# Attention weights split once, early, and reloaded as two parts

## The chip, the cores and the metric

The kernel runs on one core of one Trainium2 chip. The metric is device time in microseconds (us) of one execution. Engines are called as in the profile: PE (TensorE, its matmuls), PEld (its weight loads), DVE (VectorE), ACT (ScalarE), POOL (GpSimd) and SP (SyncE, which here only issues DMAs). A line such as L112 is line 112 of the kernel before.

## The reference

One step of a small decoder trunk, on 16 meta tokens plus 1,024 prompt tokens and on 8 sample tokens, 1,024 features wide, all in fp32:

```
hp = layer_norm(ALPHA * hp + pool_mixer(hp));   hp = layer_norm(ALPHA * hp + conv_ffn(hp))   # layer 0
k, v = hp @ w_kv + b_kv                                                                      # shared keys, values
q = x @ w_q + b_q                      # 16 heads of 64, 4 kv heads, window of 128, one sink per head
e = exp(s - m);  p = e / (sum(e) + exp(sink - m));  y = (p @ v) @ w_o + b_o
hp = layer_norm(ALPHA * hp + y);                hp = layer_norm(ALPHA * hp + conv_ffn(hp))   # layer 1

conv_ffn: g, u = split(x @ w_in);  c = conv_b + sum_k g[shifted by k] * conv_w[k];  (silu(c) * u) @ w_out
```

D_FF is 2,816, that is 22 tiles of 128. Layer 0 mixes by pooling, layer 1 by the attention.

## The kernel before

Activations lie feature-major: 8 tiles of 128 features, and columns for tokens in three chunks (280, 384 and 384 columns). Full precision on PE is had by exact parts: a matrix `w` is kept as `w_hi`, rounded to fp32r, and `w_lo = w - w_hi`, and a product is three matmuls, hi*hi, hi*lo and lo*hi (`mm3`, L115 to L122).

Weights arrive unsplit. `load_w` (L103) loads 128x1024 fp32 (512 KB) into a staging tile `raw` (two buffers), ACT rounds it into the upper half of a tile `w` (L111, CAST), and POOL subtracts to make the lower half (L112). Tiles `w` have four buffers, tiles `wo` two. With `pieces=2` both steps are done in two halves of 512 columns. All ConvFFN weights and all attention weights come this way: 2 for keys, 2 for values, 24 loads of query weights (8 head pairs in each of 3 chunks), and 24 loads of output weights (8 in each of 3 chunks).

The ConvFFN (L354) runs over tiles f = 0..21. `ffn1(f, c)` makes gate and value products of one chunk on PE (L365, L367); ACT copies the gate out of PSUM (L376, L390); POOL makes the first term of the convolution (L378, L392); DVE adds the other terms (L393, L394); ACT takes Silu (L398); DVE multiplies (L399); ACT rounds and DVE subtracts for the parts of `h` (L401, L402). After every second f, `ffn2` (L405) multiplies two tiles of h by two output weights into 8 sums per chunk, and DVE adds each PSUM bank into `acc` (L417 to L420). Six PSUM banks serve both.

The attention (L589 to L862) runs units of 128 queries of one head pair: scores, masked minimum on DVE (L645), exp on ACT (L647), normalization on DVE (L650), transposes, split (L660, L661), and the product with the values (L676 to L683). Beside them run the query projection of the next head pair (L607, with four small SBUF-to-SBUF DMAs `q<-q`, L623 and L628) and the output projection of the chunk (`pz`, L757).

The order of the instructions on each engine is made by a planner: it simulates the program with its own costs and places every instruction when its simulated engine and operands come free. On the chip each engine then works strictly in that order, waiting on semaphores. All DMAs are issued by SP, in SP's order.

Of the kernel before, what the change touches and what calls it, by code (L numbers as in the profile page):

```python
# [7 lines left out]
F32 = mybir.dt.float32  # L8
# [19 lines left out]
# prompt blocks (of 128 tokens) per chunk; the first chunk also carries the  # L28
# meta tokens and the sample tokens: columns [meta 16 | samples 8 | prompt]
# [6 lines left out]
# columns alive after the attention: [meta14 meta15 | samples 8 | prompt]  # L36
# [3 lines left out]
# packed per-partition constant columns  # L40
# [7 lines left out]
# constants of the first phase alone  # L48
# [11 lines left out]
def trunk_kernel(ctx: ExitStack, tc: tile.TileContext, ins: dict, outs: dict):  # L60
# [19 lines left out]
    # ------------------------------------------------------------ constants  # L80
# [33 lines left out]

    def mm3(out, wts, movs):  # L115
        """out += sum_k w_k^T x_k over exact hi/lo parts (all but lo*lo)."""
        n = len(wts)
        for k in range(n):
            (wh, wl), (mh, ml) = wts[k], movs[k]
            nc.tensor.matmul(out, lhsT=wh, rhs=mh, start=(k == 0), stop=False)  # L120
            nc.tensor.matmul(out, lhsT=wh, rhs=ml, start=False, stop=False)  # L121
            nc.tensor.matmul(out, lhsT=wl, rhs=mh, start=False, stop=(k == n - 1))  # L122
# [7 lines left out]
    # ----------------------------------------------------------- layer norm  # L130
    def colsum(parts, W, name, on_pe, own=False, split=False, pairs=False, step=KT):
        """mean over all features of 8 [P, W] tiles -> PSUM, on every partition; pauses after every step tiles."""
        ps = bank(f"ps_{name}", "ln")[:, :W]
        if on_pe:
            # fp32 products; with pairs, of sums of two tiles
            n = KT // 2 if pairs else KT
            for k in range(n):
                if pairs:
                    t = hslot([P, W], f"pr{k}_{name}", F32)
                    (nc.gpsimd if k < n // 2 else nc.vector).tensor_tensor(t, parts(2 * k), parts(2 * k + 1), ALU.add)  # L140
                else:
                    t = parts(k)
                nc.tensor.matmul(ps, lhsT=r32(ones), rhs=t, start=(k == 0), stop=(k == n - 1))
            return ps
        s = [None, None]
        for m in range(0, KT, 2):
            # two chains of sums, so that one is ready while the other's last ends
            i = m // 2 % 2
            a, b = parts(m), parts(m + 1)
            eng = nc.vector if split and i else nc.gpsimd  # L150
            if s[i] is None:
                s[i] = a if own else ltmp([P, W], f"s{i}_{name}")
                eng.tensor_tensor(s[i], a, b, ALU.add)
            else:
                eng.tensor_tensor(s[i], s[i], a, ALU.add)
                eng.tensor_tensor(s[i], s[i], b, ALU.add)
            if (m + 2) % step == 0 and m + 2 < KT:
                yield
        s, s1 = s
        nc.gpsimd.tensor_tensor(s, s, s1, ALU.add)  # L160
        sh = ltmp([P, W], f"sh_{name}", F32R)
        sl = ltmp([P, W], f"sl_{name}", F32R)
        nc.scalar.copy(sh, s)
        nc.vector.tensor_tensor(sl, s, r32(sh), ALU.subtract)
        nc.tensor.matmul(ps, lhsT=ones, rhs=sh, start=True, stop=False)
        nc.tensor.matmul(ps, lhsT=ones, rhs=sl, start=False, stop=True)
        return ps
# [10 lines left out]
    def ln_steps(z, W, lni, c, xo, name, out=None, on_pe=False, on_pool=(), lnexp=False, split=False, fin=False):  # L178
        # a list of tiles in the place of x, which gets new ones
# [18 lines left out]
        if lnexp:  # L198
            # both functions share a table set with the softmax's
            nc.scalar.activation(rstd, var, AF.Ln, bias=epsc)  # L200
            nc.scalar.activation(rstd, rstd, AF.Exp, scale=-0.5)
        else:
            nc.scalar.activation(rstd, var, AF.Sqrt, bias=epsc)
            nc.vector.reciprocal(rstd, rstd)
# [37 lines left out]
    # ------------------------------------------------------------ first loads  # L242
# [29 lines left out]
    # ------------------------------------------------------------ pool mixer  # L272
    def pool_chunk(c):
# [22 lines left out]
        def rest(g):  # L296
# [9 lines left out]
            if c == 0:  # L306
                # samples: last w-1 state rows and the token itself
                if w == 2:
                    nc.vector.tensor_tensor(dsm[:, ks], spl[:, ks, :, 2], xst[:, ks], ALU.add)
                else:  # L310
                    st = spl[:, ks] if g == 1 else spt[:, 2 * g - 4:2 * g - 2, :, 16 - w:]
                    nc.vector.tensor_reduce(dsm[:, ks], st, AX.X, ALU.add)
                    nc.vector.tensor_tensor(dsm[:, ks], dsm[:, ks], xst[:, ks], ALU.add)
                nc.vector.scalar_tensor_tensor(dt[:, :, NMETA:NMETA + NS], dsm[:, ks], 1.0 / w, xst[:, ks], ALU.mult, ALU.subtract)
            yield
            # alpha * x
# [12 lines left out]
        for g in range(4):  # L329
            # in this order on the vector engine, whose first groups' loads land first  # L330
            with tc.issue_after(last[g - 1]) if c == 0 and g else nullcontext():
                if g < 3:
                    sums(g)
                r = rest(g)
                next(r)
            next(r, 0)
# [5 lines left out]
    # ------------------------------------------------------------------- FFN  # L342
# [11 lines left out]
    def ffn(L, first_w):  # L354
# [67 lines left out]
        def ffn2_last(gi, c):  # L422
            """the last group: the sums of its first half run while the second half's h is made."""
# [38 lines left out]
        gi = 0  # L462
        for f in range(3, NF - 2):
            win[f + 1] = load_in(f + 1)
            for c in range(NCH):
                ffn1(f, c, *win[f])
            if f == 3 or f % 2 == 0:
                for c in range(NCH):
                    ffn2(gi, c)
                gi += 1  # L470
                load_wo(2 * gi)
                load_wo(2 * gi + 1)
        win[NF - 1] = load_in(NF - 1)
        lns = []
        for c in range(NCH):
# [7 lines left out]
            if c == NCH - 1:  # L483
                exp_tables()
                # the reciprocal root of the chunk before shares this chunk's table set
                for _ in lns[0]:
                    if L == 1:
                        break
# [18 lines left out]
    # ---------------------------------------------------------- phase 1: pool  # L507
# [14 lines left out]
    # ------------------------------------------------- pass-through state rows  # L522
# [7 lines left out]
    # ------------------------------------------------------------ shared K / V  # L530
# [9 lines left out]
    wk = [load_w(ins["wk"][i], f"wk{i}") for i in range(2)]  # L540
    wv = [load_w(ins["wv"][:, 1024 * i:1024 * (i + 1)], f"wv{i}") for i in range(2)]
# [46 lines left out]
    # --------------------------------------------------------------- attention  # L588
    O = {}  # L589

    class Q:
        """query projection of head pair t for one chunk, issued in slices."""
# [19 lines left out]
        def finish(self):  # L612
# [5 lines left out]
            # one engine after the other: they take turns at a bank  # L618
# [11 lines left out]
    def att_s(u, q):  # L630
# [10 lines left out]
        # e = -s with the negated sink as its last column, mx = -max  # L641
# [43 lines left out]
    def load_state(i):  # L685
        """state keys and values of kv heads 2i and 2i+1; slot 0 holds the new token."""
# [7 lines left out]
    def att_virtual(i, kv):  # L694
        """the 8 samples and the last two meta tokens, for kv heads 2i and 2i+1."""
# [49 lines left out]
    def o_weights(c, half, mp):  # L745
        return load_w(ins["wo"][half, mp], f"wo_{c}_{half}_{mp}", pieces=2)

    def o_piece(c, half, m, w, z):
        """half of the output projection's sum, for output tile m."""
# [6 lines left out]
        if half == 0:  # L756
# [3 lines left out]
            # the sum takes the place of x  # L760
# [5 lines left out]
    def later_kv():  # L766
        """the later chunks' keys and values, made beside the first units."""
# [16 lines left out]
    # slots of 512 columns for the transposed weights; the first query weights pass through  # L784
# [3 lines left out]
    wq = {0: load_w(ins["wq"][0], "wq0", pieces=2, w=early)}  # L788
# [11 lines left out]
    # output projection: (first unit, chunk, half, tile); the weights of a pair of tiles come ahead  # L800
# [21 lines left out]
    for n in range(len(units) + LAG_V + 1):  # L822
        if n < len(units):
            c, t, j = units[n]
            h = heads.index((c, t))
            if h + 1 < len(heads):
                nc_, nt_ = heads[h + 1]
                if j == 0:
                    wq[h + 1] = load_w(ins["wq"][nt_], f"wq{h + 1}", pieces=2, w=early if h == 0 else None)
                    qs[nc_, nt_] = Q(nc_, nt_, wq[h + 1])  # L830
# [46 lines left out]
def _lay_out(inputs):  # L877
# [5 lines left out]
    def fm(x):  # L883
        """[tokens, features] -> [partition, feature tile, token]"""
        return x.T.reshape(-1, P, x.shape[0]).transpose(1, 0, 2)
# [19 lines left out]
    # heads in pairs: pair 4c+g holds head g of kv head 2c, then of kv head 2c+1  # L905
# [3 lines left out]
    # [half of the pairs, pair of output tiles, partition, (output tile, head pair, column)]  # L909
# [19 lines left out]
    # constants of the shapes alone  # L929
# [46 lines left out]
```

## Time and profile before

| | |
|---|---|
| median of 3 runs | 2004.76 us (2003.29 to 2010.54) |
| profiled execution, first to last instruction | 2004.4 us |
| first ConvFFN, from its steady part to its end | about 120 to 820 us |
| keys, values, attention, its layer norm | about 820 to 1230 us |
| second ConvFFN | about 1230 to 1990 us |
| PE busy | 1932.9 us (96%) |
| DVE, ACT, POOL busy | 1263.3, 712.3, 813.9 us |
| HBM read and written | 108.29 and 7.54 MB |

The profiled execution's span and the median agree to 0.4 us, so the two can be used as one. [...]

### The profile page before, as it was taken

What the parts mean: (1) busy time and instruction counts of PE and PEld (TensorE: products, weight loads), DVE (VectorE), ACT (ScalarE), POOL (GpSimd) and SP (SyncE); (2) the same over time, 40 slices, a digit from 0 to 9 for tenths busy, and PEclk for the clock granted to TensorE, in tenths of its full rate; (3) what the DMA queues carried; (4) which work ended last, traced back from release to release, by engine and by line L of the source; (5) the groups of instructions that cost most, each with busy time, mean ns of one, the idle gap of its engine ahead of it and who ended that gap; (6) DMA issues with size and microseconds to landing.
All of it is one profiled execution on the core that took longest, in us unless ns stands there. A gap on an engine that the chain in (4) does not pass through costs nothing. (4 is left out here: it accounts for less than half of the span.)

```text
span 2004.4 us, 31349 instructions
## 1 busy us (share of the span) xinstructions
PE 1932.9 (96%) x12208; PEld 1896.3 (95%) x12208; DVE 1263.3 (63%) x2367; ACT 712.3 (36%) x1585; POOL 813.9 (41%) x880
## 2 busy tenths in 40 slices
PE   6899999999999999899999989999999999999997
PEld 4699999999999999889999988999999999999996
DVE  7977545454544456887989896675445454544566
ACT  2452122112211221476778784512122112212234
POOL 6752334214321432653464657533143224322333
PEclk9899999999999999999999999999999999999998
DMA  5201111101110111314343322011011011101102
GB/s 194 78 22 43 53 54 63 43 22 64 64 37 27 64 53 34 30 49 148 107 132 102 109 81 85 32 51 55 33 64 55 31 42 63 54 32 43 64 23 65
DMA packets 50422, 123.45 MB, mean 62 GB/s; under 512 B 11481, under 2 KB 25489, under 8 KB 50217
## 3 DMA queue, kind: packets, MB, share of 16 engines
q1 hardware_dynamic: 50272, 121.44, 19.6%
q8 instruction: 96, 1.57, 0.3%
q14 instruction: 54, 0.43, 0.1%
HBM read 108.29 MB, written 7.54 MB: 58 GB/s over the span
## 5 line engine op out<-in xcount | busy, mean ns | idle before, releaser
L112 POOL TENSOR_TENSOR w_wo<-raw_wo,w_wo 128x512 fp32r<-128x512 f32 (+1 forms) x92 | 169.3, 1859 | 550.9 <-ACT w_wo L111 548.0
L121 PE MATMUL pg<-xl,w_g 128*128 128x384 f32 (+2 forms) x1056 | 337.4, 319 | 0.0
L121 PE MATMUL pu<-xl,w_u 128*128 128x384 f32 (+2 forms) x1056 | 336.6, 319 | 0.0
L420 DVE TENSOR_TENSOR acc<-acc,po 128x384 f32<-128x384 f32 (+2 forms) x432 | 222.1, 515 | 173.8 <-PE po L122 170.9
L121 PE MATMUL po<-h,w_wo 128*128 128x384 f32 (+2 forms) x960 | 305.9, 319 | 0.0
L120 PE MATMUL po<-h,w_wo 128*128 128x384 f32 (+2 forms) x960 | 305.7, 318 | 0.0
L122 PE MATMUL po<-h,w_wo 128*128 128x384 f32 (+2 forms) x960 | 305.6, 318 | 0.0
L111 ACT CAST w_wo<-raw_wo 128x512 fp32r<-128x512 f32 (+1 forms) x92 | 71.6, 822 | 422.4 <-PE po L122 417.6
L402 DVE TENSOR_TENSOR h<-c,h 128x280 fp32r<-128x280 f32 (+2 forms) x132 | 147.7, 1119 | 88.3 <-ACT h L401 87.7
L392 POOL TENSOR_SCALAR c<-g,cols 128x384 f32<-128x384 f32 (+1 forms) x110 | 80.2, 729 | 294.6 <-issue 281.6
L121 PEld LDWEIGHTS pg<-xl,w_g 128*128 128x128 f32 x1056 | 198.8, 188 | 0.1
L121 PEld LDWEIGHTS pu<-xl,w_u 128*128 128x128 f32 x1056 | 198.3, 188 | 0.0
L393 DVE SCALAR_TENSOR_TENSOR c<-g,cols,c 128x384 f32<-128x384 f32 (+1 forms) x110 | 67.8, 616 | 194.4 <-POOL c L392 194.4
L122 PEld LDWEIGHTS po<-h,w_wo 128*128 128x128 f32 x960 | 180.4, 188 | 0.0
L120 PEld LDWEIGHTS po<-h,w_wo 128*128 128x128 f32 x960 | 180.3, 188 | 0.0
L121 PEld LDWEIGHTS po<-h,w_wo 128*128 128x128 f32 x960 | 180.1, 188 | 0.0
L398 ACT ACTIVATE c<-c 128x280 f32<-128x280 f32 (+2 forms) x132 | 65.1, 493 | 312.4 <-DVE c L394 277.5
L120 PE MATMUL pg<-xh,w_g 128*128 128x384 f32 (+1 forms) x528 | 170.1, 322 | 0.0
L122 PE MATMUL pg<-xh,w_g 128*128 128x384 f32 (+1 forms) x528 | 169.1, 320 | 0.0
L120 PE MATMUL pu<-xh,w_u 128*128 128x384 f32 (+1 forms) x528 | 168.9, 320 | 0.0
L122 PE MATMUL pu<-xh,w_u 128*128 128x384 f32 (+1 forms) x528 | 168.8, 320 | 0.0
L120 PE MATMUL pg<-xa,w_g 128*128 128x384 f32 (+1 forms) x528 | 168.6, 319 | 0.0
(270 smaller groups left out, 4673.5 us busy)
## 6 DMA issues: line engine op xcount, KB each, us to landing
raw_g<-in_win SPq DMA_DIRECT2D x44, 512.0 KB, 3.5
raw_u<-in_win SPq DMA_DIRECT2D x44, 512.0 KB, 3.5
raw_wo<-in_wout SPq DMA_DIRECT2D x44, 512.0 KB, 3.5
raw_wq<-in_wq SPq DMA_DIRECT2D x24, 512.0 KB, 3.5
raw_wo<-in_wo SPq DMA_DIRECT2D x24, 512.0 KB, 3.6
q<-q SPq DMA_DIRECT2D x64, 96.0 KB, 2.1
praw<-in_xq SPq DMA_DIRECT2D x8, 400.0 KB, 5.4
out_yT<-acc SPq DMA_DIRECT2D x8, 384.0 KB, 2.5
```

The lines of the kernel that those rows point to most:

```text
L111: nc.scalar.copy(w[:, 0, s], raw[:, s])
L112: nc.gpsimd.tensor_tensor(w[:, 1, s], raw[:, s], r32(w[:, 0, s]), ALU.subtract)
L120: nc.tensor.matmul(out, lhsT=wh, rhs=mh, start=(k == 0), stop=False)
L121: nc.tensor.matmul(out, lhsT=wh, rhs=ml, start=False, stop=False)
L122: nc.tensor.matmul(out, lhsT=wl, rhs=mh, start=False, stop=(k == n - 1))
L392: nc.gpsimd.tensor_scalar(cc, g[:, 0:n], w0, b, ALU.mult, ALU.add)
L393: nc.vector.scalar_tensor_tensor(cc, g[:, 1:1 + n], w1, cc, ALU.mult, ALU.add)
L398: nc.scalar.activation(ct, ct, AF.Silu)
L402: nc.vector.tensor_tensor(ht[:, 1, :], ct, r32(ht[:, 0, :]), ALU.subtract)
L420: nc.vector.tensor_tensor(a, a, ps, ALU.add)
```

## The change

A DRAM tile `parts` holds 20 weights of the attention in two parts of 128x1024 each. A generator `split_parts` fills it during the first ConvFFN: each weight goes in three pieces of columns (384, 384, 256), so 60 pieces. For a piece SP loads the columns, ACT rounds them, POOL subtracts, and SP stores the upper and the lower part. The three small tiles of a piece come from the tag `lt`, which has five buffers. The code asks for four pieces at each f from 3 on. In the attention `load_parts` loads both parts at once (1 MB) straight into the tile `w`; nothing is left for ACT and POOL to do on it. The rest of the diff drops comments.

```
+    parts = tc.dram_tile([20, P, 2, 1024], F32, name="parts")
+    OWK, OWV, OWQ, OWO = 0, 2, 4, 12
+    def split_parts():
+        srcs = [ins["wk"][i] for i in range(2)] + [ins["wv"][:, 1024 * i:1024 * (i + 1)] for i in range(2)]
+        srcs += [ins["wq"][i] for i in range(8)] + [ins["wo"][i // 4, i % 4] for i in range(8)]
+        for i, src in enumerate(srcs):
+            for a, e in ((0, 384), (384, 768), (768, 1024)):
+                raw = ltmp([P, e - a], f"sr{i}_{a}")
+                nc.sync.dma_start(raw, src[:, a:e])
+                hi = ltmp([P, e - a], f"sh{i}_{a}", F32R)
+                nc.scalar.copy(hi, raw)
+                lo = ltmp([P, e - a], f"sl{i}_{a}", F32R)
+                nc.gpsimd.tensor_tensor(lo, raw, r32(hi), ALU.subtract)
+                nc.sync.dma_start(parts[i][:, 0, a:e], r32(hi))
+                nc.sync.dma_start(parts[i][:, 1, a:e], r32(lo))
+                yield
+    def load_parts(i, name, tag="w", w=None):
+        if w is None:
+            w = pool.tile([P, 2, 1024], F32R, tag=tag, bufs={"w": 4, "wo": 2}[tag], name=f"w_{name}")
+        nc.sync.dma_start(r32(w), parts[i])
+        return w
...
+        ahead = split_parts() if L == 0 else iter(())
         for f in range(3, NF - 2):
             win[f + 1] = load_in(f + 1)
+            for _ in range(4):
+                next(ahead, 0)
...
-    wk = [load_w(ins["wk"][i], f"wk{i}") for i in range(2)]
-    wv = [load_w(ins["wv"][:, 1024 * i:1024 * (i + 1)], f"wv{i}") for i in range(2)]
+    wk = [load_parts(OWK + i, f"wk{i}") for i in range(2)]
+    wv = [load_parts(OWV + i, f"wv{i}") for i in range(2)]
...
-        return load_w(ins["wo"][half, mp], f"wo_{c}_{half}_{mp}", pieces=2)
+        return load_parts(OWO + 4 * half + mp, f"wo_{c}_{half}_{mp}")
...
-    wq = {0: load_w(ins["wq"][0], "wq0", pieces=2, w=early)}
+    wq = {0: load_parts(OWQ, "wq0", w=early)}
...
-                    wq[h + 1] = load_w(ins["wq"][nt_], f"wq{h + 1}", pieces=2, w=early if h == 0 else None)
+                    wq[h + 1] = load_parts(OWQ + nt_, f"wq{h + 1}", w=early if h == 0 else None)
```

What it does to the order is seen at three places. In the names, `h0_3_2` is h of layer 0, f = 3, chunk 2; `sr`, `sh` and `sl` with a weight's number and a first column are a piece's raw, upper and lower tile; the line numbers of the change are its own.

ACT, from the last cast of f = 3 to the first gate copy of f = 4, before:

```order
L401 CAST h0_3_2_1490<-c0_3_2_1480 128x384
L111 CAST w_wo0_2_1714<-raw_wo0_2_1712 128x1024
L111 CAST w_wo0_3_1719<-raw_wo0_3_1717 128x1024
L374 COPY g0_4_0_1783<-pg0_4_0_1732 128x16
L375 COPY gs_69<-pg0_4_0_1732 128x8
```

and in the change:

```order
L427 CAST h0_3_2_1525<-c0_3_2_1515 128x384
L128 CAST sh5_768_2889<-sr5_768_2887 128x256
L128 CAST sh6_0_2897<-sr6_0_2895 128x384
L128 CAST sh6_384_2905<-sr6_384_2903 128x384
L128 CAST sh6_768_3117<-sr6_768_3115 128x256
L128 CAST sh7_0_3125<-sr7_0_3123 128x384
L128 CAST sh7_384_3133<-sr7_384_3131 128x384
L128 CAST sh7_768_3141<-sr7_768_3139 128x256
L128 CAST sh8_0_3555<-sr8_0_3553 128x384
L111 CAST w_wo0_2_1749<-raw_wo0_2_1747 128x1024
L111 CAST w_wo0_3_1754<-raw_wo0_3_1752 128x1024
L128 CAST sh8_384_3563<-sr8_384_3561 128x384
```

Eight pieces stand between the two casts that followed each other before, and a ninth ahead of the gate copy of f = 4, which is the next row. All 60 pieces lie between the Silu of f = 1 in chunk 1 and the cast of output weight 6.

POOL, around the first convolution term of f = 3 in chunk 2, before:

```order
L389 COPY g0_3_2_1481<-carry_68 128x2
L392 TENSOR_SCALAR c0_3_2_1480<-g0_3_2_1481,cols_61 128x384
L395 COPY carry_68<-g0_3_2_1481 128x2
L373 MEMSET g0_4_0_1783 128x2
L112 TENSOR_TENSOR w_wo0_2_1714<-raw_wo0_2_1712,w_wo0_2_1714 128x1024
```

and in the change:

```order
L418 TENSOR_SCALAR c0_3_1_1452<-g0_3_1_1453,cols_61 128x384
L130 TENSOR_TENSOR sl4_384_2453<-sr4_384_2449,sh4_384_2451 128x384
L415 COPY g0_3_2_1516<-carry_68 128x2
L130 TENSOR_TENSOR sl4_768_2461<-sr4_768_2457,sh4_768_2459 128x256
L130 TENSOR_TENSOR sl5_0_2469<-sr5_0_2465,sh5_0_2467 128x384
L418 TENSOR_SCALAR c0_3_2_1515<-g0_3_2_1516,cols_61 128x384
```

The convolution term now stands behind the lower parts of three pieces.

SP, around the loads of output weights 0 and 1, before:

```order
L105 DMA raw_wo0_0_1279<-in_wout 128x1024
L105 DMA raw_wo0_1_1284<-in_wout 128x1024
L105 DMA raw_g0_4_1289<-in_win 128x1024
L105 DMA raw_u0_4_1294<-in_win 128x1024
L105 DMA raw_wo0_2_1712<-in_wout 128x1024
```

and in the change:

```order
L131 DMA parts_102<-sh1_384_1769 128x384
L126 DMA sr1_768_1775<-in_wk 128x256
L105 DMA raw_wo0_0_1282<-in_wout 128x1024
L132 DMA parts_102<-sl1_384_1771 128x384
L131 DMA parts_102<-sh1_768_1777 128x256
L126 DMA sr2_0_1783<-in_wv 128x384
L105 DMA raw_wo0_1_1287<-in_wout 128x1024
L132 DMA parts_102<-sl1_768_1779 128x256
L131 DMA parts_102<-sh2_0_1785 128x384
L126 DMA sr2_384_1791<-in_wv 128x384
```

Per piece SP now has a store of the upper part, the load of the next piece and a store of the lower part, in this cycle, and the ConvFFN's own loads stand among them.

## Rows read from the trace of the kernel before

**Rows 1.** The page's first part: span, and busy time of PE.

```profile
span 2004.4 us, 31349 instructions
PE 1932.9 (96%) x12208; PEld 1896.3 (95%) x12208; DVE 1263.3 (63%) x2367; ACT 712.3 (36%) x1585; POOL 813.9 (41%) x880
```

**Rows 2.** Busy time by stretch; columns as in the first row.

```profile
core 0: us, PE busy (x) PEld busy (x) DVE busy (x) ACT busy (x) POOL busy (x), PEclk, DMA share, GB/s
836.00:840.50 4.50, 0.75 (x5) 0.43 (x3) 3.64 (x4) 1.91 (x4) 2.51 (x3) 1.00 0.51 6
840.50:843.90 3.40, 2.79 (x9) 2.74 (x9) 3.40 (x3) 2.18 (x3) 3.32 (x3) 0.51 0.81 30
120.00:320.00 200.00, 200.00 (x1254) 200.00 (x1253) 121.81 (x186) 49.06 (x92) 69.53 (x73) 1.00 0.14 46
320.00:820.00 500.00, 497.04 (x3136) 496.46 (x3135) 257.34 (x408) 111.80 (x220) 163.76 (x183) 1.00 0.14 46
820.00:1230.00 410.00, 383.89 (x2627) 375.29 (x2626) 359.56 (x938) 297.85 (x783) 226.63 (x257) 0.97 0.35 98
```

**Rows 3.** PE's waits, 820 to 1230 us: total, times, longest.

```profile
PE tp L658 <- DVE e L650: 4.0, 2, 3.6
PE av L676 <- DVE ring L661: 2.9, 2, 1.6
...
PE s L639 <- DMA q<-q: 1.6, 2, 0.8
PE s L639 <- DVE mx L645: 1.2, 1, 1.2
```

**Rows 4.** Timeline of ACT, four instructions: start, duration, line, idle before.

```profile
121.38 0.53 ACT L398 ACTIVATE c<-c 128x384 f32<-128x384 f32 x1
...
176.37 0.51 ACT L401 CAST h<-c 128x384 fp32r<-128x384 f32 x1 [1.51 <-DVE c L399]
198.09 2.00 ACT L111 CAST w_wo<-raw_wo 128x1024 fp32r<-128x1024 f32 x2 [21.21 <-PE po L122]
...
312.25 2.00 ACT L111 CAST w_wo<-raw_wo 128x1024 fp32r<-128x1024 f32 x2 [21.16 <-PE po L122]
```

**Rows 5.** DMA issues: count, KB each, median us from issue to landing.

```profile
raw_wo<-in_wout SPq DMA_DIRECT2D x44, 512.0 KB, 3.5
...
q<-q SPq DMA_DIRECT2D x64, 96.0 KB, 2.1
out_yT<-acc SPq DMA_DIRECT2D x8, 384.0 KB, 2.5
...
out_ncs<-gs SPq DMA_DIRECT2D x2, 88.0 KB, 3.6
...
out_kp<-kout SPq DMA_DIRECT2D x2, 64.0 KB, 2.6
```

**Rows 6.** Groups of ACT by form, 120 to 320 us: count, busy, mean ns.

```profile
L401 ACT CAST h<-c 128x384 fp32r<-128x384 f32 x13 | 6.7, 512 | 9.4 <-DVE c L399 9.4
...
L376 ACT COPY g<-pg 128x256 f32<-128x256 f32 x5 | 2.0, 392 | 0.0
```

**Rows 7.** Groups of POOL by form, 120 to 320 us.

```profile
L112 POOL TENSOR_TENSOR w_wo<-raw_wo,w_wo 128x1024 fp32r<-128x1024 f32 x8 | 19.9, 2502 | 80.8 <-ACT w_wo L111 80.7
```

**Rows 8.** Timeline of SP, one issue: start, duration.

```profile
201.87 0.33 SPq L105 DMA_DIRECT2D raw_g<-in_win  x1
```

**Rows 9.** Groups of POOL by form, 850 to 1230 us.

```profile
L112 POOL TENSOR_TENSOR w_wo<-raw_wo,w_wo 128x512 fp32r<-128x512 f32 x48 | 63.0, 1331 | 32.2 <-ACT w_wo L111 29.4 <-issue 2.6
L112 POOL TENSOR_TENSOR w_wq<-raw_wq,w_wq 128x512 fp32r<-128x512 f32 x44 | 57.0, 1308 | 34.1 <-ACT w_wq L111 27.2 <-issue 6.8
```

**Rows 10.** Groups of ACT by form, 850 to 1230 us.

```profile
L111 ACT CAST w_wo<-raw_wo 128x512 fp32r<-128x512 f32 x48 | 27.4, 617 | 4.8 <-PE pz L122 3.6 <-DMA raw_wo<-in_wo 0.9
```

**Rows 11.** Groups of DVE by form, 850 to 1230 us.

```profile
L650 DVE TENSOR_SCALAR e<-e,mx 128x256 f32<-128x256 f32 x128 | 64.9, 548 | 1.2
```

**Rows 12.** Timeline of DVE and of POOL, 1058 to 1060 us.

```profile
1058.54 1.20 DVE L650 TENSOR_SCALAR e<-e,mx 128x256 f32<-128x256 f32 x2
...
1059.84 0.35 DVE L650 TENSOR_SCALAR e<-e,mx 128x256 f32<-128x256 f32 x1
...
1058.57 0.75 POOL L155 TENSOR_TENSOR sq_m<-sq_m,sq_m 128x266 f32<-128x266 f32 x1
```

## The prediction, on record before the result

> **What bounds the kernel now.** I read the page first: PE is busy 96% of 2004.4 us [rows 1]. Then busy time by stretch [rows 2]. In the first ConvFFN PE works 200.0 of 200 us and 497.0 of 500 at full clock, with every other engine far from full: nothing can be gained there, and whatever makes PE wait there is lost. In the stretch of the attention PE works 383.9 of 410 us at a mean clock of 0.97, and DVE 359.6 (88%). So 26.1 us of idle PE and 0.03 x 410 = 12.3 us of clock, 38 us together, are all that the attention could give back. Third, PE's waits there [rows 3]: of those with a clear owner DVE has the largest, 4.0 + 2.9 + 1.2 = 8.1 us; copies of q cost 1.6 us. [...] A change is worth what it does to waits in these two stretches. The median of the runs is 0.4 us from the profiled span, so I sum on the span and add 0.4.
>
> **First ConvFFN: what is added.** 60 loads, 120 stores, 60 casts on ACT and 60 subtractions on POOL. As busy time this is little. A cast of 384 columns takes 0.51 us, one of 256 about 0.39 [rows 6]: 40 x 0.51 + 20 x 0.39 = 28 us of ACT, busy 49 of 200 us. POOL takes 2.50 us for 1024 columns [rows 7] and 1.33 for 512 [rows 9], on that line 1.04 for 384 and 0.75 for 256: 57 us, beside 70 of 200. What counts is where they stand. The code asks for four pieces per f, but in the order all 60 lie between the Silu that ends at 121.9 us and the cast of output weight 6 at 312.25 [rows 4]: 190 us, 3.17 us a piece. Eight pieces fill the hole of 21.2 us that ACT has behind the last cast of f = 3 [rows 4]: 2.65 us a piece.
>
> How long a piece takes on the chip follows from SP's cycle: store upper n, load n+1, store lower n, store upper n+1. The load of the next piece is issued only behind the store of this one's upper part, and that store waits for this piece's cast. So the chain of one piece is landing + cast + one issue. A load of 192 KB lies between the copy of 96 KB (2.1 us) and the load of 512 KB (3.5) [rows 5]: by straight line 2.42 us, 2.21 for 128 KB. An issue is 0.33 us [rows 8]. That is 2.42 + 0.51 + 0.33 = 3.26 us for 384 columns and 2.21 + 0.39 + 0.33 = 2.93 for 256; 40 and 20 of these make 189 us. That alone fills the 190. Into the same stretch fall the splits of 16 weights of the ConvFFN itself (gates and values 3 to 7, output weights 0 to 5). Each puts a POOL subtraction of 2.50 us [rows 7] where a piece's lower part may have to wait for it, and the store of that lower part stands ahead of the next upper store on SP. It costs the chain between 0 (inside the landing of a load) and 2.50; I take the middle, 1.25 x 16 = 20 us. So the last piece ends 189 + 20 - 190 = 19 us late.
>
> PE gets this through the queues, which are strict. On POOL the first convolution term of f = 3, chunk 2, stands behind three pieces; DVE's terms wait for it; behind those on DVE stand the sums that empty the PSUM banks of `po`; and PE stops in `ffn2` when its six banks are full. On ACT the casts of output weights and the gate copies of the next f stand behind eight or nine pieces. There are three such groups in the stretch (behind f = 3, 4 and 6), each with a stop and so a half-speed stretch of 1.7 us: 5 us. The ConvFFN loses 19 + 5 = 24 us. From both sides: with every load landing in 2.1 us and every split of a weight hidden, the pieces take 174 us and nothing is lost (nor gained, since PE has no idle time to give back). With 3.5 us a load and 2.50 a weight it is 258 + 40 - 190 = 108 us, and 5. The small copies are far nearer in size than the 512 KB load, so I stay by them.
>
> **Attention: what goes.** POOL loses the 92 halves listed, 120 us [rows 9], four more for the first query weights and four full ones for keys and values; ACT loses 96 casts of 0.617 us, 59 us [rows 10]. Neither is what PE waits for most; the gain is on DVE. The normalization L650 takes 0.548 us in the mean [rows 11], but 0.35 with nothing on POOL; the two that share their time with POOL's 0.75 us addition take 1.20 together [rows 12]. POOL's layer norm work stays, the splits are most of the rest: at best 128 x (0.548 - 0.350) = 25 us of DVE. How much PE sees of it lies between nothing and the 38 us above; nearer ends are the 8.1 us that PE visibly waits for DVE and the 25 us of relief. I take their middle, 17 us. The loss of the subtractions also takes 0.62 + 1.33 us from a weight's way into `w`, but the load now waits for the tile `w` itself, no longer for a staging tile; I let these cancel. If the cover is gone, that is up to 24 x 2 us of waiting for weights, the upper end here.
>
> **Attention: what is added.** 48 loads and the four for keys and values are twice as long. From 96 to 512 KB a load gains 1.4 us, so another 512 KB about 1.7: landing at 5.2 us. Behind such a load on the same queue stand the four small copies of q, without which the next head pair's scores can't start; PE waits for them twice now [rows 3]. I take that a quarter of the 24 head pairs loses 0.7 us: 4 us, between 0 and 24 x 1.7 = 41.
>
> **Sum.** 2004.4 + 24 - 17 + 4 + 0.4 = 2016 us.
>
> **Rivals.**
> 1. The pieces fit, and the change is faster. For it: ACT is idle 151 of 200 us and POOL 130 [rows 2], and the copies of q land in 2.1 us. It decides from a mean pace under 3.17 us a piece, weights included. Then the ConvFFN loses nothing, and 2004.8 - 17 + 4 = 1992. Against: 2.93 us is already the shortest piece by rows 5, without any weight.
> 2. The pieces nearly fit: half of the weights' cost is hidden, 9 us late and two half-speed stretches, 12 us lost and 13 returned: 2004, no change.
> 3. The attention returns nothing: the relief of DVE moves its idle time only, since three DVE waits of 8.1 us in all are what PE shows [rows 3], while the large loads cost 4 us: 2004.8 + 24 + 4 = 2033.
> 4. The stores, not the loads, set the pace. The load of piece n+2 needs the buffer of the upper part of n, so two pieces take at least landing + cast + store landing. With 2.5 or 2.6 us a store [rows 5] that is 2.42 + 0.51 + 2.6 = 5.5 us, 2.8 a piece, no bound. One kind of store lands in 3.6 us [rows 5] and would come to 3.27, still level. At 4.5 us a store it would be 3.7 a piece, 0.55 x 60 = 33 us more: 2049. [...]
>
> **Chances.** A run is told from no change from about 0.5%, 10 us: faster below 1995, slower above 2015. The forecast (2008 to 2028) has 0.55, of which 0.13 lies within the bound; rival 1 has 0.10, rival 2 0.13, rival 3 0.15, rival 4 0.07. Slower is 0.42 + 0.15 + 0.07 = 0.64, the same 0.13 + 0.13 = 0.26, faster 0.10. For 8 in 10 I go from 1996 (half of rival 1 left out) to 2043 (between rivals 3 and 4). The likeliest case by itself is 2008 to 2028.
>
> **What would show it.** Right: PE idle between 120 and 350 us, where it had none, with three clusters in `po`, DVE named as the one waited for, and half-speed stretches behind them; f = 8 reached some 24 us later; the pieces 3.2 to 3.6 us apart in ACT's timeline; L650 near 0.4 us in the mean; the stretch from the end of the first ConvFFN to the start of the second 10 to 17 us shorter; the second ConvFFN as before. Wrong: PE without a gap at f = 3 to 7 (then rival 1 or 2); stores to `parts` landing after 4 us (rival 4); PE waiting in the attention for weights or copies of q (rival 3); or idle PE in the second ConvFFN, which nothing here touches.

## The result, and the profile after

The changed kernel takes 2055.64 us in the median (2053.66 to 2057.57, four runs) for 2005.11 before (2003.29 to 2010.54, four runs). The ratio is 1.0234 (95% interval 1.0217 to 1.0251): slower by 2.3%, 40 us above the 2016 of the forecast and outside its range.

The page's first part, as [rows 1], shows a longer span and hardly more work on PE:

```profile
span 2055.8 us, 31703 instructions
...
PE 1942.9 (95%) x12208; PEld 1903.5 (93%) x12208; DVE 1228.9 (60%) x2367; ACT 681.6 (33%) x1545; POOL 737.0 (36%) x840
```

DVE, ACT and POOL are all less busy than before, and the kernel is slower. Busy time by stretch, as [rows 2], says where (PEclk is the clock that PE was granted, as a share of full speed):

```profile
core 0: us, PE busy (x) PEld busy (x) DVE busy (x) ACT busy (x) POOL busy (x), PEclk, DMA share, GB/s
150.00:200.00 50.00, 38.33 (x224) 37.44 (x223) 20.13 (x32) 14.64 (x30) 23.97 (x28) 0.83 0.54 164
200.00:250.00 50.00, 43.11 (x261) 42.50 (x260) 24.56 (x46) 11.10 (x22) 22.22 (x21) 0.97 0.53 163
250.00:300.00 50.00, 44.04 (x249) 43.20 (x249) 17.48 (x33) 11.10 (x23) 19.91 (x21) 0.86 0.47 147
300.00:350.00 50.00, 35.33 (x204) 33.65 (x202) 21.23 (x26) 15.07 (x34) 24.35 (x30) 0.83 0.53 163
...
870.00:1285.00 415.00, 387.88 (x2658) 379.92 (x2659) 330.88 (x948) 244.02 (x687) 98.37 (x163) 0.98 0.52 162
```

PE had no idle time between 120 and 320 us; now it has 39 us of it in 200, at a lower clock. By the starts of the same matmuls in the two timelines, all but 1.7 us of the loss arises in the three `ffn2` groups: chunk 1's sum of the first group starts 17.6 us later than before, that of the second 35.2, that of the third 55.4. From there to f = 20 the distance stays 55.4 (801.9 us for 746.5), at the first product of the keys it is 52.0, at the start of the second ConvFFN 54.5, at the end of the span 51.4. So 3.4 us come back at the end of the first ConvFFN, and 2.5 are lost again between the keys and the second ConvFFN: the attention with what leads up to it returned 0.9 us against this one profile of before (e1 shows how far that carries). The 3.4 come with a wait that [rows 3] leave out. In the view that these rows are taken from it is the first row, and a second one is left out too:

```profile
PE po L433 <- DVE c L399: 4.4, 1, 4.4
...
PE pk L121 <- DVE xl L233: 3.1, 1, 3.1
```

The first is the stop ahead of the half-speed stretch of [rows 2]; in the change PE stops for 0.5 us at that place.

In the attention POOL's busy time fell from 226.6 to 98.4 us and DVE's from 359.6 to 330.9. The normalization (L650 before, L679 now) is as light as foreseen; group of DVE by form, 870 to 1285 us, to be read against [rows 11]:

```profile
L679 DVE TENSOR_SCALAR e<-e,mx 128x256 f32<-128x256 f32 x128 | 45.7, 400 | 1.2
```

But PE's waits there (total, times, longest) have a new head, to be read against [rows 3]:

```profile
PE s L668 <- DMA q<-q: 9.4, 6, 3.1
PE pq L636 <- DMA w_wq<-parts: 4.0, 3, 1.6
...
PE pq L636 <- DMA ring<-parts: 2.7, 1, 2.7
PE pv L606 <- DMA w_wv<-parts: 2.4, 1, 2.4
```

DVE's two largest waits of [rows 3] (4.0 and 2.9 us) are gone, and 18.5 us of waits for transfers stand in their place. How the copies of q come to be late is seen in SP's timeline (start, duration):

```profile
957.08 0.32 SPq L138 DMA_DIRECT2D w_wq<-parts  x1
957.74 1.11 SPq L652 DMA_DIRECT2D q<-q  x2
```

A load of 1 MB is issued 0.66 us ahead of them. It is no exception: by SP's timeline a large load is issued less than 1.5 us ahead of the first copy in 20 of the 24 head pairs (11 times one of output weights), where it was 2 before, of 512 KB. The copies land in 5.3 us, against 2.1 in [rows 5]; DMA issues, 870 to 1285 us:

```profile
w_wq<-parts SPq DMA_DIRECT2D x22, 1024.0 KB, 5.4
q<-q SPq DMA_DIRECT2D x64, 96.0 KB, 5.3
```

What the ConvFFN waits for is read from the back. PE's waits, 120 to 380 us:

```profile
PE po L146 <- DVE c L425: 21.9, 8, 5.5
PE po L146 <- ACT g L416: 14.1, 4, 6.0
PE po L146 <- DVE acc L446: 3.7, 2, 2.4
```

DVE and ACT are named, but neither was near full (20.1 and 14.6 of 50 us in the first of the four rows above). The chain of waits through 201 to 210 us (start, duration, what) shows who held them:

```profile
201.14 0.52 ACT sh L128
...
201.68 0.32 SPq L131
...
202.09 3.60 DMA sr<-in_wq
...
205.79 0.53 ACT sh L128
206.33 0.32 SPq L131
...
206.75 3.03 DMA sr<-in_wq
```

This is the cycle of the prediction: cast, issue of the upper store, landing of the next load, cast. Its sizes are not those predicted. DMA issues, 118 to 380 us, against [rows 5]:

```profile
parts<-sh SPq DMA_DIRECT2D x40, 192.0 KB, 2.4
parts<-sl SPq DMA_DIRECT2D x40, 192.0 KB, 2.8
...
sr<-in_wq SPq DMA_DIRECT2D x16, 192.0 KB, 2.8
sr<-in_wo SPq DMA_DIRECT2D x16, 192.0 KB, 3.1
...
sr<-in_wq SPq DMA_DIRECT2D x8, 128.0 KB, 3.0
sr<-in_wo SPq DMA_DIRECT2D x8, 128.0 KB, 2.9
```

A load lands in 2.98 us in the mean of these medians and those of wk and wv, weighted by their counts, where 2.42 and 2.21 were taken. Two more things can be read from the timelines of SP and ACT. The upper store of every piece is issued 0.03 us behind its cast, so no lower store that waited for POOL ever stood in its way. Between an upper store and the next load other issues stand six times, for 4.6 us in all. So POOL's subtractions hardly held the chain. The loads of the ConvFFN's own weights go with a slower one: of the 59 pieces behind the first, 16 have such a load of 512 KB issued in the 3.6 us ahead of theirs or beside it, and take 3.96 us from the issue of the load to the cast; the other 43 take 3.08.

ACT's timeline (start, duration) gives the whole stretch, against [rows 4]:

```profile
122.05 0.50 ACT L128 CAST sh<-sr 128x384 fp32r<-128x384 f32 x1
...
376.10 0.41 ACT L128 CAST sh<-sr 128x256 fp32r<-128x256 f32 x1 [3.19 <-DMA sr<-in_wo]
376.41 1.99 ACT L111 CAST w_wo<-raw_wo 128x1024 fp32r<-128x1024 f32 x2
```

60 pieces take 376.4 - 122.05 = 254.4 us, 4.24 us each; the cast that stood at 312.25 stands at 376.41, 64.2 us later. PE lost 55.4 of these; the other 8.8 did not reach it.

### The profile page after: what moved, and what is told of

Read it like the earlier page. It is cut to its first block, busy times and chain, and to the rows that moved or that the text cites. A ratio compares the mean times of both kernels' runs of the same rounds, so it can differ in the third digit from the quotient of the medians.

```text
span 2055.8 us, 31703 instructions
## 1 busy us (share of the span) xinstructions
PE 1942.9 (95%) x12208; PEld 1903.5 (93%) x12208; DVE 1228.9 (60%) x2367; ACT 681.6 (33%) x1545; POOL 737.0 (36%) x840
## 4 chain that ended last, share of the span: by engine, by line
PE 72%; DMA 11%; DVE 6%; issue 3%; ACT 3%; POOL 1%; SPq 1%; ACTq 0%; DVEq 0%; POOLq 0%
PE pg L146 7%; PE pg L148 7%; PE pg L147 7%; PE pu L147 7%; PE pu L146 7%; PE pu L148 7%; PE po L146 6%; PE po L147 6%; PE po L148 6%; DMA sr<-in_wq 3%; PE pq L636 3%; DMA sr<-in_wo 2%; DMA q<-q 1%; PE av L705 1%; DMA w_wq<-parts 1%
## 5 line engine op out<-in xcount | busy, mean ns | idle before, releaser
L146 PE MATMUL po<-h,w_wo 128*128 128x384 f32 (+2 forms) x960 | 312.1, 325 | 39.6 <-DVE c L425 21.9
L147 PE MATMUL po<-h,w_wo 128*128 128x384 f32 (+2 forms) x960 | 310.1, 323 | 0.0
L148 PE MATMUL po<-h,w_wo 128*128 128x384 f32 (+2 forms) x960 | 309.8, 323 | 0.0
L112 POOL TENSOR_TENSOR w_wo<-raw_wo,w_wo 128x1024 fp32r<-128x1024 f32 x44 | 105.9, 2425 | 438.5 <-ACT w_wo L111 438.4
L146 PEld LDWEIGHTS po<-h,w_wo 128*128 128x128 f32 x960 | 184.3, 192 | 43.7 <-DVE c L425 24.0
L148 PEld LDWEIGHTS po<-h,w_wo 128*128 128x128 f32 x960 | 184.6, 192 | 0.0
L147 PEld LDWEIGHTS po<-h,w_wo 128*128 128x128 f32 x960 | 184.4, 192 | 0.0
L146 PE MATMUL pg<-xa,w_g 128*128 128x384 f32 (+1 forms) x528 | 168.2, 319 | 0.0
L148 PE MATMUL pg<-xa,w_g 128*128 128x384 f32 (+1 forms) x528 | 168.1, 318 | 0.0
L148 PE MATMUL pu<-xa,w_u 128*128 128x384 f32 (+1 forms) x528 | 167.6, 317 | 0.0
```

Source lines behind the costliest of these rows:

```text
L112: nc.gpsimd.tensor_tensor(w[:, 1, s], raw[:, s], r32(w[:, 0, s]), ALU.subtract)
```

## The experiments

Theory A: the loss is the pace of pieces packed into one stretch, and the attention's lighter DVE is paid back by the 1 MB loads. Rivals: the pieces cost their time wherever they stand, or the attention holds a gain or loss of its own that the late ConvFFN hides.

**e1, the pieces alone.** The attention loads and splits as before:

```diff
-        return load_parts(OWO + 4 * half + mp, f"wo_{c}_{half}_{mp}")
+        return load_w(ins["wo"][half, mp], f"wo_{c}_{half}_{mp}", pieces=2)
...
```

> The pieces are made and stored in the first ConvFFN as in the change; the attention loads and splits its weights as before, so the parts are written and never read. Theory A (the chain of pieces sets the whole loss; the attention's part of the change is worth next to nothing): the stretch up to f = 20 stays 55 us late, the attention runs as before, 2005 + 54 = 2059 us (2055 to 2062). Rival B (the attention of the change really gained 17 us by the lighter DVE, and something else behind the first ConvFFN hides it): the gain goes too, and the time is 2070 us or more.

Measured: 2059.21 us, 1.0256 (1.0236 to 1.0276), the ConvFFN 50.0 us late, 5 less than theory A said. By the time theory A holds: this half of the change is the whole loss, within the noise. No gain of 17 us went missing with the other half, which speaks against rival B. Its attention is that of before in the same order on every engine, and yet e1 loses 6.3 us more between f = 20 and the second ConvFFN against the profile of before (e6 3.6, e7 8.6, with the same attention). So that profile is a fast one there, and against these three the change's attention returned not 0.9 us but 4.5 to 9.5.

**e2, the 1 MB loads alone.** No pieces; every load reads one array of both parts:

```diff
-        ahead = split_parts() if L == 0 else iter(())
...
-        nc.sync.dma_start(r32(w), parts[i])
+        nc.sync.dma_start(r32(w), parts)
```

> No pieces in the first ConvFFN; the attention loads 1 MB for each weight from one array of both parts, which one store of 1 MB writes from the first gate weight. It leaves out the right weights of the attention (all are that gate weight), so only its times count. Theory A (relief of DVE eaten by 1 MB loads that copies of q wait behind): 2001 to 2005 us, copies of q landing near 5 us, normalization of the softmax near 0.40 us in the mean. Rival B (relief reaches the end when the first ConvFFN is undisturbed): 1988 us. Rival C (the large loads cost more than the relief): 2012 us or more.

Measured: 2000.69 us, 0.9974 (0.9958 to 0.9990); copies of q land in 5.2 us, the normalization takes 0.400. So the other half gains 7 us (2007.63 before in this set), a little more than theory A had, and within the 4.5 to 9.5 above. On PE, DVE and SP its instructions stand in the order of the change.

**e3, the pieces spread.** The same 60 pieces, four behind the casts of each f:

```diff
-            for _ in range(4):
-                next(ahead, 0)
             for c in range(NCH):
                 ffn1(f, c, *win[f])
+                with tc.issue_after(mk[f, c]):
+                    for _ in range(2 if c == 0 else 1):
+                        next(ahead, 0)
```

(`mk[f, c]` is ACT's cast of h.)

> The change, but the casts of the pieces stand on ACT behind the h casts of f = 3 to 17, two behind chunk 0 and one behind each of the others, so four per f instead of eight to eleven in a row. Theory A (the loss comes from the pieces packed into 190 us at 4.1 us each): with four pieces (16 us) in an f of over 24 us the chain has slack, the ConvFFN loses 0 to 8 us, total 2002 to 2010 us, no half-speed stretch before 750 us. Rival B (the pieces' traffic and engine time cost the ConvFFN its time wherever they stand): PE still stops in the ConvFFN, total 2030 us or more.

Measured: 2001.72 us, 0.9972 (0.9962 to 0.9983). Two of its stretches:

```profile
300.00:350.00 50.00, 50.00 (x315) 50.00 (x314) 26.12 (x36) 14.25 (x30) 24.25 (x25) 1.00 0.35 115
350.00:500.00 150.00, 150.00 (x950) 150.00 (x948) 73.05 (x115) 37.85 (x79) 60.58 (x71) 1.00 0.34 109
```

PE is full at full clock beside all the loads, casts, subtractions and stores, and reaches f = 20 only 0.3 us later than before. The loads land no sooner than in the change (192 KB of wq and wo in 3.1 to 3.2 us, from 118 to 700), but nothing on PE waits for them. So the pieces cost nothing by themselves that shows in the noise (2001.7 us with them, 2000.7 without in e2); their place cost 55 us. The four calls per f in the change's code did not hold the pieces there; an order against an instruction of that f did.

**e4, copies of q on a queue of their own.** ACT issues them:

```diff
-                nc.sync.dma_start(r32(self.q2[os_, i, :]), r32(hi))
+                nc.scalar.dma_start(r32(self.q2[os_, i, :]), r32(hi))
...
```

> The change, but the four copies of q are issued by ACT on its own queue, so that they no longer stand behind a 1 MB load on SP's. Theory A (copies of q queued behind the large loads eat the attention's gain): they land in 2.1 to 2.5 us instead of 5.3, PE's 9.4 us of waiting for them go, and of the 17 us of relief 9 to 13 arrive: 2043 to 2047 us, the first ConvFFN still 55 us late. Rival B (late weights, not copies of q, are what PE waits for): 2053 to 2056 us. Rival C (ACT loses more by issuing than PE gains): 2058 us or more.

Measured: 2051.50 us, 1.0226 (1.0211 to 1.0241), between A and B. The trace decides. DMA issues, 860 to 1280 us:

```profile
w_wq<-parts SPq DMA_DIRECT2D x22, 1024.0 KB, 5.8
q<-q ACTq DMA_DIRECT2D x64, 96.0 KB, 5.4
```

The copies are as late as on SP's queue, so theory A fails at its first step: it isn't the queue. The kernel is 47.7 us late at f = 20 and 46.5 at the start of the second ConvFFN: the attention returns 1.2 us, as in the change (0.9). What differs from the change is the ConvFFN, whose loss was 47.7, 50.0 and 55.4 us in e4, e1 and the change, with the same pieces and, up to 800 us, the same order of instructions on every engine. So 8 us between them are spread and not an effect of an edit.

**e5, half the bytes.** As e2, with 512 KB a load, the upper part used for both:

```diff
-        nc.sync.dma_start(r32(w), parts)
+        nc.sync.dma_start(r32(w[:, 0]), parts[:, 0])
```

> No pieces in the first ConvFFN, no splits in the attention, and only 512 KB loaded for each weight; the upper part is used for both parts. It leaves out the right weights and their lower parts, so only its times count. It prices the removal of the splits without the doubled bytes. Theory A (the relief of DVE is real, and the long loads beside copies of q eat half of it or more): copies of q land in 3 to 4 us, the attention gains 10 to 16 us, 1990 to 1996 us. Rival B (PE hardly waited for DVE at all, so the relief is worth little by itself): as with 1 MB loads, 1999 to 2003 us.

Measured: 1985.96 us, 0.9908 (0.9879 to 0.9937), better than theory A's 1990. Its attention, PE busy in the second column:

```profile
850.00:1215.00 365.00, 349.67 (x2481) 342.22 (x2480) 302.54 (x900) 230.75 (x663) 83.71 (x142) 1.00 0.36 104
```

and the row of e2, from 850 to 1230 us:

```profile
850.00:1230.00 380.00, 356.83 (x2492) 349.16 (x2491) 302.52 (x902) 229.61 (x661) 83.79 (x144) 0.98 0.51 168
```

DMA issues of e5:

```profile
w_wq<-parts SPq DMA_DIRECT2D x22, 512.0 KB, 4.4
q<-q SPq DMA_DIRECT2D x64, 96.0 KB, 4.2
```

Removing the splits is worth 21 us (2006.99 - 1985.96); the second half of the bytes costs 15 (2000.69 - 1985.96). Half of that is idle PE, 23.2 us in e2 and 15.3 in e5, the other half, by an estimate, the clock (0.98 in the row of e2 and 1.00 in that of e5, 0.02 x 380 = 7.6 us): e2 has four half-speed stretches of 3.4 us there, e5 none. The planner also ordered the attention anew for the shorter loads, which no run separates from the bytes. The copies' landing goes with that of the load in front of them: 4.2 beside 4.4, 5.2 beside 5.7 in e2.

**e6, stores on other queues.** Pieces unspread, attention as before; ACT stores the upper part, POOL the lower:

```diff
-                nc.sync.dma_start(parts[i][:, 0, a:e], r32(hi))
-                nc.sync.dma_start(parts[i][:, 1, a:e], r32(lo))
+                nc.scalar.dma_start(parts[i][:, 0, a:e], r32(hi))
+                nc.gpsimd.dma_start(parts[i][:, 1, a:e], r32(lo))
```

> Pieces as in the change, unspread, attention as before; but ACT issues the store of the upper part and POOL that of the lower, on queues of their own, so SP only issues loads and no load stands behind a store. Theory A (the chain landing + cast + issue on SP sets the pace of 4.1 us): loads run ahead as far as five buffers allow, 2.8 to 3.3 us a piece, the ConvFFN loses 0 to 15 us, 2005 to 2020 us. Rival B (DMA bandwidth or landing times themselves set it): still 4 us a piece, 2050 us or more. Rival C (POOL's issue of 60 stores takes its time from the convolution): PE stops behind POOL, 2025 to 2045 us.

Measured: 2023.05 us, 1.0087 (1.0064 to 1.0109), between theory A and rival C. The pieces run from 121.76 to 336.3 us, 3.58 each, the ConvFFN is 16 us late. Freed from the wait for the store's issue, loads run ahead and two thirds of the loss go. The pace is above the 2.8 to 3.3 expected: loads still land in 2.5 to 3.3 us there. An issue takes POOL 0.56 us, as rival C feared; whether that has a part in the 16 us left, no run separates.

**e7, small stores.** Pieces unspread, attention as before, 64 columns a store:

```diff
-                nc.sync.dma_start(parts[i][:, 0, a:e], r32(hi))
+                nc.sync.dma_start(parts[i][:, 0, a:a + 64], r32(hi[:, :64]))
...
```

> Pieces in the same order as in the change, attention as before; but each store takes 64 columns instead of 384 or 256 (the rest of the parts is not written, and nobody reads it). Theory A (loads of pieces land in 3.0 instead of 2.4 us because they follow two stores on the same DMA engines): they land in 2.4 us, 3.4 to 3.6 us a piece, the ConvFFN loses 14 to 28 us, 2020 to 2033 us. Rival B (3.0 us is the load's own time in this stretch, stores or not): 3.9 us a piece or more, 2050 to 2060 us.

Measured: 2048.74 us, 1.0210 (1.0181 to 1.0239): by the time neither theory, nearer to B. DMA issues, 118 to 380 us:

```profile
sr<-in_wq SPq DMA_DIRECT2D x16, 192.0 KB, 2.6
...
sr<-in_wo SPq DMA_DIRECT2D x16, 192.0 KB, 2.6
parts<-sh SPq DMA_DIRECT2D x60, 32.0 KB, 1.5
...
sr<-in_wq SPq DMA_DIRECT2D x8, 128.0 KB, 2.3
sr<-in_wo SPq DMA_DIRECT2D x8, 128.0 KB, 2.3
```

The landing is nearly that of the prediction (2.42 and 2.21), with smaller stores around the loads. The pieces take 3.74 us each (120.45 to 344.9), the ConvFFN is 35.7 us late, where kernels with full stores lose 47.7 to 55.4. So the edit is worth 12 to 20 us. Not all of that need be the bytes: the order is not quite that of the change, as the planner put pieces ahead of up to seven other instructions on ACT and five on POOL that they stood behind. And 3.74 - (2.5 + 0.48 + 0.33) = 0.43 us a piece, 26 us, is neither median landing nor cast nor issue.

**e8, loads behind the copies.** e3, and each 1 MB load put behind the last copies of q asked for before it:

```diff
-        nc.sync.dma_start(r32(w), parts[i])
+        with tc.issue_after(qlast[0]) if qlast else nullcontext():
+            nc.sync.dma_start(r32(w), parts[i])
```

> The spread pieces of e3 and, in the attention, each load of 1 MB put on SP's queue behind the last copies of q that the code has asked for before it. Theory A (the copies of q land late because a 1 MB load that waited for the same weight tile is issued half a microsecond ahead of them and fills all DMA engines): more than half of the copies land in 2 to 2.6 us, PE's waits for q fall from 7.6 to 2 to 4 us, 1992 to 1998 us. Rival B (loads that start later are late themselves): the waits move to the weights, 2000 to 2006 us.

Measured: 2136.02 us, 1.0652 (1.0625 to 1.0678). DMA issues of the attention, and PE's waits, 750 to 1400 us:

```profile
q<-q SPq DMA_DIRECT2D x64, 96.0 KB, 2.1
```

```profile
PE pq L640 <- DMA w_wq<-parts: 74.5, 16, 8.2
PE pz L149 <- DMA w_wo<-parts: 18.3, 5, 4.9
```

The copies land in 2.1 us again: the load ahead of them was what delayed them (in the change the DMA share was 0.92 from 958 to 961 us, behind the load issued at 957.08). But then the weights are late. Rival B is right in kind and its price was 130 us too low. Both transfers are wanted at the moment when a projection ends, which lets a tile `w` go and makes q: in either order one of them was late.

**e9 to e11, more room.** e3 with 12 of the 48 loads in the two idle staging tiles: odd output weights (e9), every second query weight (e10), the same with these loads behind copies of q (e11).

```diff
+                        wq[h + 1] = [pool.tile([P, 1024], F32R, tag="raw", bufs=2, name=f"wr{i}_{h + 1}") for i in range(2)]
```

> The spread pieces of e3, and the odd output weights of the attention go into the two staging tiles of 4 KB that the change leaves idle there (two loads of 512 KB), so 12 of 48 loads no longer take a tile `w`. Theory A (with four tiles for 48 weights of 1 MB the loads start just when a tile comes free, at the very moment when the copies of q start): more loads come earlier, PE's waits for weights and q fall from 13 us to 7 to 9, 1994 to 1999 us. Rival B (any load beside the copies costs the same, whichever tile it fills): 1999 to 2004 us, as e3.

> As e9, but with every second query weight in the two staging tiles in the place of the odd output weights. The query weights are what PE waited for in e8, 74.5 us, and a staging tile comes free a whole head pair ahead of its next load. Theory A: 1992 to 1998 us. Rival B: as e3, 1999 to 2004 us.

> As e10, and the loads into the staging tiles are put behind the copies of q of the head pair that held the tiles before. Theory A (a load that does not stand ahead of the copies, and has time to be late): a part of the copies lands in 2.1 us, PE's waits for q fall under 4 us, 1989 to 1996 us. Rival B (the other large loads still stand ahead of the copies and decide): as e10, within 2 us.

Measured: e9 2020.83 us (1.0066, 1.0045 to 1.0088), outside both theories: copies of q land in 5.8 us, PE waits 13.2 us for them, and 8.9 us for the first weights of the second ConvFFN, which need the staging tiles. e10 2002.20 us (0.9979, 0.9965 to 0.9992), rival B. e11 2031.08 us (1.0112, 1.0088 to 1.0135), neither: PE waits 2.6 us for q, but 31.5 for the weights in the staging tiles. Room for 12 of the 48 loads gained nothing over e3 in any of the three.

**e12, parts for the output weights alone.** e3, with query weights loaded into staging and split in the attention as before (36 pieces):

```diff
-                    wq[h + 1] = load_parts(OWQ + nt_, f"wq{h + 1}", w=early if h == 0 else None)
+                    wq[h + 1] = load_w(ins["wq"][nt_], f"wq{h + 1}", pieces=2, w=early if h == 0 else None)
```

> The spread pieces of e3, but only for the output weights and those of keys and values (36 pieces); the query weights are loaded with 512 KB into a staging tile and split in the attention as before. Theory A (the loads that a query projection's end lets go are the ones that hit the copies of q): copies land in 2 to 4 us, half of the splits stay on POOL, normalization near 0.47 us, and half of the relief of 21 us arrives at half of the 15 us for bytes or less: 1993 to 1999 us. Rival B (any 1 MB load costs what its splits cost): 2000 to 2005 us.

Measured: 1994.03 us, 0.9931 (0.9915 to 0.9947), the fastest of the kernels that compute everything. DMA issues of the page, and the normalization:

```profile
raw_wq<-in_wq SPq DMA_DIRECT2D x24, 512.0 KB, 3.6
q<-q SPq DMA_DIRECT2D x64, 96.0 KB, 3.9
```

```profile
L682 DVE TENSOR_SCALAR e<-e,mx 128x256 f32<-128x256 f32 x128 | 55.1, 473 | 1.1
```

The query weights' load starts when a staging tile is free, not when a projection ends: in SP's timeline none is issued less than 1.5 us ahead of a head pair's first copy of q. Loads of output weights still are, for 9 of the 24 head pairs; in the change 20 had a load there. As theory A had it, the copies are less late and the normalization is half relieved. PE's waits for q did not fall with that (9.8 us in 4 waits, 7.6 in e3), so how the 8 us between e3 and e12 divide among copies, weights, clock and the planner's new order stays open.

## Why the prediction was wrong

Over the profiled spans the ConvFFN cost 31 us more than the 24 forecast, the attention returned 12 us less than the 13 forecast (6 less by e2), and 3 us were gained behind it.

**The mechanism of the ConvFFN was right.** The chain of a piece, the place of all 60 in one stretch, the way to PE through `c`, the gate copies and `po`, three groups, the second ConvFFN nearly untouched (54.5 us late at its start, 52.9 in its last group): all as put, but for how the ConvFFN's own weights get in the way.

**The step that failed is the landing of a piece's load**, 2.42 and 2.21 us by straight line between [rows 5]. It measured 2.98. Those rows were mostly of transfers with nothing else issued just before them (69 of the 96 copies, 7 of the 8 loads of output weights between 100 and 320 us, by SP's timeline, nothing in the 3.5 us ahead); here each load is issued 0.4 us behind a store of 192 or 128 KB, and another follows while it is under way. With small stores it was 2.6 and 2.3 (e7). Against the predicted mean of 2.35 that is 60 x 0.63 = 38 us. The term for the ConvFFN's own weights was 20 us; what is left of a piece's 4.24 us after 2.98 + 0.48 + 0.33 comes to 0.45 x 60 = 27, or 7 us more. Its size was near, but not its cause: it was to come from POOL's subtractions, which hardly held the chain (4.6 us at most), and the weights' loads make up only some (3.96 for 3.08 us, in 16 pieces: 14 us). 209 + 38 + 7 = 254 us, the time measured; it must come out so, since the last term is what was left. The 8.8 us that did not reach PE were not counted.

**The half-speed stretches** were taken as 1.7 us behind each of three stops, 5 us, and came to 11 or 12. No run shows 1.7 us as the price of a stop: behind the stop of [rows 2] the granted clock was 0.51 for 3.4 us, behind those of the ConvFFN 0.50 for 17.0 to 17.1. Three rows, from each stop on:

```profile
182.33:199.29 16.96, 7.89 (x30) 7.22 (x31) 6.75 (x15) 3.56 (x8) 4.49 (x9) 0.50 0.44 140
247.10:264.20 17.10, 9.84 (x36) 8.84 (x37) 7.15 (x14) 4.12 (x10) 5.54 (x9) 0.50 0.46 141
332.40:349.50 17.10, 6.70 (x24) 5.70 (x24) 4.34 (x7) 4.31 (x10) 5.51 (x9) 0.50 0.41 131
```

Matmuls of 280 columns start 0.233 us apart there (182.73 to 183.66 us), and 0.129 at a clock of 1.00 (177.38 to 179.44). So of the 24.4 us of work some 10.9 are what it took longer, by these starts, or 12.2 by the clock alone, both estimates; with PE's waits of 40.4 us that is 51.3 to 52.6 of the 55.4. The part of the clock must not be added to the pieces' lateness, as the prediction did: in these stretches PE stood idle for 26.7 of 51.2 us, waiting for the pieces anyway.

**Attention.** The relief was put at 17 us and is worth 21 (e5). That it came so near is in part luck: its lower end, and the ground of rival 3, was "three DVE waits of 8.1 us in all". The view has 14 rows of PE waiting for DVE in that window, 21.5 us, and [rows 3] leave out two of the three largest (4.4 and 3.1). The large loads were put at 4 us; the doubled bytes cost 15 (e5 against e2). The step that failed: "a quarter of the 24 head pairs loses 0.7 us". The copies land in 5.3 us, not 2.8, and in 20 of the 24, because a load waits for the tile that the ending projection lets go and so is issued less than 1.5 us ahead of them (0.66 in the case shown). The moment of that release did not enter the sum. So of the 13 us forecast the attention returned 0.9 by the profiles and 7 by e2. By the profiles that is near rival 3's nothing, but not for its reason: the relief did reach PE (e5), and the loads took back most of it.

**Rival 4** named a time near the result (2049) with a wrong mechanism: no run shows the 4.5 us it takes for a store to `parts`; those of 192 KB land in 2.4 and 2.8 us and are not waited for. They count by standing among the loads (12 to 20 us between full and small ones, e7).

The queue was not what made the copies of q late: beside loads of 1 MB they land in 5.3 us from SP (the change) and 5.4 from ACT (e4), and in 2.1 with the loads behind them (e8). What it is in a transfer that makes the next one late, no run here shows.

Sum over the profiled spans: 2004.4 + 55.4 (ConvFFN) - 0.9 (attention) - 3.1 (behind it) = 2055.8.

## What to carry to other kernels

A small transfer's price was here not its landing in a quiet trace but that of what was issued in front of it, on either of the two queues tried: look for what lets both of them go. Work that a program asks for "four per step" can be bunched by the scheduler wherever engines are idle; read its place from the order, and pin it to an instruction of the step if the pace matters: that alone was worth 54 us here. Moving a split out of a busy stretch can cost at another place, if the bytes that replace it are wanted at the same moment as a short transfer on the path (15 us between e2 and e5): half of the weights gave more here (1994 us, e12) than all of them (2002, e3).

## What was not expected of the hardware

Half-speed stretches of 17.0 to 17.1 us behind stops in the ConvFFN, where [rows 2] had 3.4. PE went on stopping inside the first of them (6.0 us before 190.12 us). A second queue for the copies of q moved their landing by 0.1 us. And 512 KB loads next to copies of q land in 4.3 to 4.4 us (e5), not 3.5 as the same size does in the ConvFFN [rows 5].
